# Weight sums of the values' block product: from VectorE to accumulating DMAs in DRAM

## The chip, the cores and the metric

The kernel runs on one core of one Trainium2 chip. Such a core has TensorE (PE in the profile; PEld are its weight loads), VectorE (DVE), ScalarE (ACT), GpSimd (POOL) and SyncE (SP, which here only issues DMAs). Its working memory is SBUF; the matmul results stand in PSUM; weights and intermediate sums that are not in SBUF stand in DRAM. The metric is the device time of one execution in microseconds, lower is better; one execution is also profiled, and every row shown below is of that one.

## The reference, cut to what matters

One layer of a streaming encoder: 512 frames of 1024 numbers, all in float32. One combined projection of the normed input feeds attention (q, k, v), a recurrent branch (xr, gr) and two gates (ga, gb):

```python
xn = rmsnorm(h, norm_mix_g[l])
u = jnp.einsum('bsd,de->bse', xn, w_in[l])
q, k, v, xr, gr, ga, gb = jnp.split(u, splits, axis=-1)
ya = chunked_band_attention(q, k, v, rel_table[l]) @ w_attn_out[l]
xc = causal_depthwise_conv(xr, conv_w[l], conv_b[l])
hr = rg_lru(xc, ...)
yb = (hr * jax.nn.gelu(gr)) @ w_rnn_out[l]
...
h = h + (g_a * ya + g_b * yb) @ w_o[l]
...
h = h + (jax.nn.silu(g) * up) @ w_ffn_out[l]
```

The change concerns `v`, the product of `xn` (512 x 1024) with the 1024 columns of `w_in` for the values.

## The kernel before

**Split numbers.** Every float32 operand of a product is held as two parts, a high one (rounded to TensorE's fast float32 form) and a low one, the rest. `split` (L84 to L87) makes them: ACT writes the high part (L86), DVE subtracts it from the source (L87). A product is three matmuls (`mm3`, L80 to L82): high by high, high by low, low by high.

**Weights.** The weights arrive in chunks, in the order of a list (`plan`). A chunk is loaded by SP into "raw" tiles of 512 KB, of which there are three buffers, and split into "whl" tiles, of which there are four. `weights(name, ahead)` gives a chunk and loads and splits as many as `ahead` further ones. An SP load whose buffer is not free waits at SP, and everything behind it on SP waits too.

**Order of work.** Where nothing else is said, a planner decides the order of the instructions on each engine, by what it expects to be ready; each engine then runs its own list strictly in order. `tc.keep_in_program_order(x)` ties one instruction behind the instruction that was written just before it on its engine; those written after it are not tied. In the values' product and in attention, PE's order is as written.

**The stages around the change.**

- The recurrent loop, `for j in range(0, KT, 2)`, runs over j = 0, 2, 4, 6. Each pass handles two feature tiles: the products xr and gr, the convolution (`rnn_conv`, its POOL part is L764, which writes the low half of `xch`), the gate products `rg` (L793, which read `xch`), the gates and the scan (`gates_of`, its POOL parts are L817 and L831, the low half of the recurrent output), and the products ga and gb, whose gate is applied by ACT (`gate`, into `ta` and `zB`). After j = 2, 4, 6 `sums_kept` (L319 to L340) loads blocks of other weights, sums them on DVE and stores the sums to DRAM for later stages.
- Then q and k tiles of the first heads, and the output projection of the recurrent branch, `yb` (eight products, the result into `zB` at L1152). Between them stand the scores of heads 0 and 1 (L1076 to L1087) and `x_sums` (L979, L981), which forms four sums of blocks of `xn` for the values' product.
- Then the values' product, `v_all`: the 2 x 2 blocks of `xn` and of the values' weights are multiplied by a scheme of seven block products in place of eight. Weights of three of them are blocks as they are (`w11`, `w22`, `w21`), and of four are sums of blocks (`t1` to `t4`). The seven run in the order w11, t1, t2, w22, t3, w21, t4, each 24 matmuls of 512 columns. The results are kept, added (L1032) and split again.
- Then attention over 16 heads, the merge, the product with `w_o`, and the feed-forward part.

**The sums before the change.** With the blocks B11, B12, B22, B21 of the values' weights, in two halves u = 0, 1 of 128 x 1024 numbers each: `v_weight_sums(u)`, called in the `yb` loop after its products j = 3 and j = 5, loads B11, B12 and B22 (`v_raw`, L283, two DMAs of 256 KB to a tile) and forms t1 = B12 - B11 (L291) and t2 = B22 - t1 (L292) on DVE, into SBUF tiles that stay. `v_weights` takes t1 and t2 from there; for t3 it loads B11 again and subtracts it from t2 (L306); for w21 it also turns t2 into t4 = B21 - t2 in place (L310).

A like scheme by DMAs stands in the kernel for the last stage already: `out_copy` (L224) copies a block within DRAM from SP, `out_add` (L233) adds another to it by an accumulating DMA from POOL, sometimes after a POOL copy of one column (L230) that makes POOL wait for some other engine's result.

Of the kernel before, what the change touches and what calls it, by code (L numbers as in the profile page):

```python
# [8 lines left out]
F32 = mybir.dt.float32  # L9
F32R = mybir.dt.float32r  # L10
AF = mybir.ActivationFunctionType
ALU = mybir.AluOpType
PSUM = bass.MemoryType.PSUM

P = 128
D = 1024
S = 512
KT = D // P
NT = S // P
# [10 lines left out]
C_Q, C_K, C_V, C_XR, C_GR, C_GA, C_GB = (i * D for i in range(7))  # L30
# [12 lines left out]
def block_kernel(ctx: ExitStack, tc: tile.TileContext, x, norm_mix_g, w_in, b_merge, rel_table,  # L43
# [230 lines left out]
        high_first(hl[:, 0], hl[:, 1], raw[:])  # L274
        return lambda part, k, at=every: hl[:, part, k, at]

    v_t1, v_t2 = [], []

    def v_raw(kind, kh, half, u):
        raw = wp.tile([P, 2, S], F32, tag="raw", bufs=3, name=f"raw_v_{kind}_{kh}{half}{u}")  # L280
        at = kh * S + u * CW
        for n, gr in enumerate(v_groups[half]):
            sp.dma_start(out=raw[:, :, n * CW:(n + 1) * CW],  # L283
                         in_=w_in[at:at + CW, C_V + gr * CW:C_V + (gr + 1) * CW].rearrange("(k p) e -> p k e", p=P))
        return raw[:]

    def v_weight_sums(u):

        b11, b12, b22 = v_raw("t", 0, 0, u), v_raw("t", 0, 1, u), v_raw("t", 1, 1, u)
        t1, t2 = (aw.tile([P, 2, S], F32, tag="v", bufs=4, name=f"v_t{n}_{u}")[:] for n in (1, 2))  # L290
        dve.tensor_sub(t1, b12, b11)  # L291
        dve.tensor_sub(t2, b22, t1)  # L292
        v_t1.append(t1)
        v_t2.append(t2)

    def v_weights(kind):

        hl = [wp.tile([P, 2, 2, S], F32R, tag="whl", bufs=4, name=f"whl_v_{kind}_{u}") for u in range(2)]
        for u in range(2):
            if kind == "t1":  # L300
                src = v_t1[u]
            elif kind in ("t2", "t4"):
                src = v_t2[u]
            elif kind == "t3":
                src = v_raw(kind, 0, 0, u)
                tc.keep_in_program_order(dve.tensor_sub(src, v_t2[u], src))  # L306
            else:
                src = v_raw(kind, int(kind[1]) - 1, int(kind[2]) - 1, u)
                if kind == "w21":
                    dve.tensor_sub(v_t2[u], src, v_t2[u])  # L310
            split(hl[u][:, 0], hl[u][:, 1], src)
        return lambda part, k: hl[k // 2][:, part, k % 2]

# [453 lines left out]
    def rnn_conv(j, po_xr):  # L767
        xc = conv_in(j, po_xr)
        conv_taps(j, po_xr, xc)
        return xc, conv_out(j, xc)  # L770
# [67 lines left out]
    def gates_of(j):  # L838
        pos = [rnn_gate_products(j + c, conv[j + c][1], ("s", "mm")[c]) for c in range(2)]
        for c in range(2):  # L840
            xc, _, g = conv.pop(j + c)
            held.append(rnn_gates(j + c, xc, pos[c], g))
        act.activation(u_pairs[-1][:], u_pairs[-1][:], AF.Sqrt, scale=-1.0)
        while held:
            rnn.append(rnn_scan(*held.pop(0)))

    def tile_of(name, c, tag="mm", ahead=1):

        whl = weights(name, ahead)
        if (name, c) in first:  # L850
            po = first[name, c]
            project(po, whl, c, xnT, 256, S)
        else:
            po = mm_tile(f"po_{name}_{c}", tag)
            project(po, whl, c, xnT)
        return po
# [13 lines left out]
    def gate(w, j):  # L870
        po = tile_of(f"g{'ab'[w]}{j - j % 2}", j % 2, "t" if j < 2 and w == 0 else "mm")
        act.activation((ta, zB)[w][j], po[:], AF.Tanh, bias=hb[:, 16 + 8 * w + j:17 + 8 * w + j], scale=0.5)
# [20 lines left out]
    for j in range(0, KT, 2):  # L893
        if j:
            for c in range(2):
                conv[j + c] = rnn_conv(j + c, tile_of(f"xr{j}", c, ahead=2))
        for c in range(2):
            if j:
                po = tile_of(f"gr{j}", c, "t")
                conv[j + c] += (rnn_gelu(j + c, po),)  # L900
        if j:
            gates_of(j)
        for w in range(j // 4, 2):
            for c in range(2):
                gate(w, j + c)
            if j == w == 0:
                gates_of(j)
        if j:
            sums_kept(obp, "oof"[j // 2 - 1], (0, 1, 0)[j // 2 - 1])

# [52 lines left out]
    def x_block(half, kh, part):  # L963
        return xn_all[:, 4 * kh:4 * kh + 4, part, half * 256:half * 256 + 256]

    def x_sums():

        s, s3 = (zp.tile([P, 4, 256], F32, tag="late", bufs=2, name=f"v_s{n}")[:] for n in (1, 3))
        out = {}

        def parted(key, src):
            pl, tag = (aw, "v") if key == "s4" else (aw2, "pt")
            hi, lo = (pl.tile([P, 4, 256], F32R, tag=tag, bufs=4, name=f"v_{key}{n}") for n in "hl")
            split(hi[:], lo[:], src)
            out[key] = hi, lo

        def chain(dst, first_, *rest):
            (op, one, two) = first_
            tc.keep_in_program_order(op(dst, one, two))  # L979
            for op, one in rest:  # L980
                op(dst, dst, one)  # L981

        add, sub = dve.tensor_add, dve.tensor_sub
        chain(s, (add, x_block(1, 0, 0), x_block(1, 1, 0)), (add, x_block(1, 0, 1)), (add, x_block(1, 1, 1)))
        parted("s1", s)
        chain(s, (sub, s, x_block(0, 0, 0)), (sub, x_block(0, 0, 1)))
        parted("s2", s)
        chain(s3, (sub, x_block(0, 0, 0), x_block(1, 0, 0)), (add, x_block(0, 0, 1)), (sub, x_block(1, 0, 1)))
        chain(s, (sub, x_block(0, 1, 0), s), (add, x_block(0, 1, 1)))
        return out, parted, s, s3  # L990

    def v_pairs(gr, half):
# [12 lines left out]
    def v_all(sums):  # L1005
        out, parted, s, s3 = sums
        x_, y_ = ([mm_tile(f"v_{n}{a}", tag) for a in range(2)] for n, tag in (("x", "mm"), ("y", "t")))
        z_ = [mm_tile(f"v_z{a}") for a in range(2)]

        def product(banks, kind, rows, start):  # L1010
            w = weights(f"v_{kind}")
            for a in range(2):
                for k in range(4):
                    if isinstance(rows, str):
                        hi, lo = (o[:, k, a * P:(a + 1) * P] for o in out[rows])
                    else:
                        hi, lo = (x_block(*rows, part)[:, k, a * P:(a + 1) * P] for part in range(2))
                    mm3(banks[a][:], hi, lo, w(0, k), w(1, k), start and k == 0, k == 3, parts=True)

        def keep(o, banks):  # L1020
            for a in range(2):
                act.activation(o[:, a], banks[a][:], AF.Copy)

        def given(half, side, src):
            for a in range(2):
                for n, gr in enumerate(v_groups[side]):
                    v = vs[gr][2 * half + a]
                    split(v[:, :, 0::3], v[:, :, 1:3], src(a)[:, n * CW:(n + 1) * CW].rearrange("p (a b d) -> p a b d", a=2, b=2))

        def summed(o, banks, half, side):  # L1030
            for a in range(2):
                dve.tensor_add(o[:, a], banks[a][:], o[:, a])  # L1032
            for gr in v_groups[side]:
                v_pairs(gr, half)
            given(half, side, lambda a: o[:, a])

        product(x_, "w11", (0, 0), True)
        keeps = [rnp.tile([P, 2, 2, S], F32, tag="big", bufs=4, name=f"v_keep{n}") for n in range(2)]
        v_big.append(rnp.tile([P, 2, 2, S], F32R, tag="big", bufs=4, name="v_big"))
        x1, x2, z1 = keeps[0][:, 0], keeps[0][:, 1], keeps[1][:, 0]  # L1040
        keep(x1, x_)
        product(z_, "t1", "s1", True)
        keep(z1, z_)
        parted("s4", s)
        product(x_, "t2", "s2", False)
        keep(x2, x_)
        parted("s3", s3)
        product(z_, "w22", "s4", False)
        summed(x2, z_, 0, 1)
        product(x_, "t3", "s3", False)  # L1050
        summed(z1, x_, 1, 1)
        product(y_, "w21", (0, 1), True)
        summed(x1, y_, 0, 0)
        product(x_, "t4", (1, 1), False)
        for gr in v_groups[0]:
            v_pairs(gr, 1)
        given(1, 0, lambda a: x_[a][:])
# [87 lines left out]
    for j in range(KT):  # L1145
        if j in (4, 6):
            probs[j // 2 - 2] = scores(j // 2 - 2)
        po = mm_tile(f"po_yb{j}")
        project(po, weights(f"yb{j - j % 2}"), j % 2, rnn)
        if j in (3, 5):  # L1150
            v_weight_sums(j // 2 - 1)
        dve.scalar_tensor_tensor(zB[j], zB[j], 1.0, po[:], ALU.add, ALU.mult)  # L1152
    with tc.manual_schedule(engines={mybir.EngineType.PE}):
        v_all(sums)
# [582 lines left out]
```

## Time and profile before

| what | us |
|---|---|
| median of three runs | 847.26 |
| lowest and highest of the three | 846.86, 848.89 |
| the profiled execution | 848.82 |
| its span, first to last instruction | 847.0 |
| TensorE busy in the span | 837.2 |
| VectorE busy | 654.1 |
| ScalarE busy | 524.3 |
| GpSimd busy | 159.9 |

The rows that follow are of the profile's page and of answers of its trace. A row of a group of instructions gives line, engine, operation, output and inputs by the program's names, the count, the durations in ns, and the first and last start in us. A row of a timeline gives start and duration in us; in brackets stands how long the engine was idle before, and what ended that. "SPq" is the issue of a DMA by SP, not its transfer; the "landing" is the time from the issue until the data have arrived. A row by stretches gives, for each engine, busy time and count of instructions, then the granted TensorE clock, the busy share of the 16 DMA engines and the GB/s they moved.

### The profile page before, as it was taken

The page shows a single profiled execution, that of the slowest core. Times are in us where ns is not written, and L with a number is a line of the kernel's source. Part 1 is how long each engine was busy: PE and PEld are TensorE (multiplying, and loading weights), DVE is VectorE, ACT ScalarE, POOL GpSimd, SP SyncE. Part 2 cuts the span into 40 slices and gives each one's busy share as a digit, 9 for nine tenths or more (in the row PEclk, how much of TensorE's full clock was granted, in tenths as well). Part 3 has the DMA queues.
Part 4 walks back from the last instruction along what each step waited for, and adds up shares of the span by engine and source line. Part 5 has one row for each costly group of instructions (what it writes and reads, how often), then busy time and mean ns, then how long its engine had stood idle before and what let it go on. Part 6 is the DMA issues. An engine that isn't in the chain of part 4 may idle for free.

```text
span 847.0 us, 11664 instructions
## 1 busy us (share of the span) xinstructions
PE 837.2 (99%) x4102; PEld 708.8 (84%) x4102; DVE 654.1 (77%) x960; ACT 524.3 (62%) x868; POOL 159.9 (19%) x207
## 2 busy tenths in 40 slices
PE   9999999999999999999999999999999999999996
PEld 6988888888878888888888888888888999988885
DVE  6667779886999778777568777889777878599784
ACT  7595848773456678878544469663765466555543
POOL 2412030221040043343211000005102322200000
PEclk9999999999999999999999999999999999999998
DMA  8433386687565444549448984555955576455442
GB/s 286 166 103 117 130 298 243 212 271 243 167 205 150 132 134 148 157 152 223 94 132 211 320 294 154 157 187 166 229 176 159 150 187 207 140 177 168 160 165 99
DMA packets 104058, 153.96 MB, mean 182 GB/s; under 512 B 8024, under 2 KB 62896, under 8 KB 103488
## 3 DMA queue, kind: packets, MB, share of 16 engines
q1 hardware_dynamic: 99040, 141.32, 51.2%
q0 software_dynamic: 3728, 8.96, 6.4%
q10 hardware_dynamic: 1232, 2.95, 0.9%
q8 instruction: 32, 0.52, 0.3%
q14 instruction: 26, 0.21, 0.1%
HBM read 139.53 MB, written 30.45 MB: 201 GB/s over the span
## 4 chain that ended last, share of the span: by engine, by line
PE 84%; DVE 7%; ACT 4%; DMA 3%; issue 2%; ACTq 0%; DVEq 0%
PE fu_x L80 2%; PE fu_x L81 2%; PE fu_x L82 2%; PE o L1122 2%; PE fg_x L82 2%; PE fg_x L80 2%; PE fg_x L81 2%; PE pT L1102 2%; PE po_ga L82 2%; PE po_ya L80 2%; PE po_ya L82 2%; PE p_out L81 2%; PE p_out L80 2%; PE po_ya L81 2%; PE p_out L82 2%
## 5 line engine op out<-in xcount | busy, mean ns | idle before, releaser
L1326 POOL TENSOR_TENSOR sg<-sg,keep_fu_x 128x512 f32<-128x512 f32 (+1 forms) x10 | 17.8, 1784 | 163.4 <-DVE keep_fu_x L1325 163.4
L1091 POOL TENSOR_SCALAR p<-p,rl 128x128 f32<-128x128 f32 (+3 forms) x61 | 43.8, 733 | 13.7 <-DVE rl L1087 9.4
L1085 DVE CUSTOM_DVE_ANT_0 p<-s,bias 128x128 f32<-128x128 f32 (+1 forms) x64 | 28.6, 486 | 12.6 <-PE s L1077 11.1
L1086 ACT ACTIVATE p<-p,m 128x128 f32<-128x128 f32 (+1 forms) x64 | 35.5, 555 | 2.3 <-DVE m L1085 2.0
L87 DVE TENSOR_TENSOR whl_fu_w<-raw_fu_w,whl_fu_w 128x1024 fp32r<-128x1024 f32 (+1 forms) x18 | 22.1, 1230 | 9.0 <-ACT whl_fu_w L86 9.0
L87 DVE TENSOR_TENSOR pp<-pT,pp 128x384 fp32r<-128x384 f32 (+1 forms) x48 | 26.9, 595 | 2.0 <-ACT pp L86 1.8
L81 PE MATMUL po_xr<-xnT,whl_xr 128*128 128x512 f32 (+1 forms) x80 | 27.7, 354 | 0.0
L87 DVE TENSOR_TENSOR whl_fu_t<-t_fu,whl_fu_t 128x1024 fp32r<-128x1024 f32 (+1 forms) x18 | 23.2, 1293 | 5.9 <-ACT whl_fu_t L86 5.7
L81 PE MATMUL po_gr<-xnT,whl_gr 128*128 128x512 f32 (+1 forms) x80 | 27.5, 347 | 0.0
L82 PE MATMUL po_gr<-xnT,whl_gr 128*128 128x512 f32 (+1 forms) x80 | 27.3, 347 | 0.0
L82 PE MATMUL po_xr<-xnT,whl_xr 128*128 128x512 f32 (+1 forms) x80 | 27.3, 347 | 0.0
L80 PE MATMUL po_gr<-xnT,whl_gr 128*128 128x512 f32 (+1 forms) x80 | 27.2, 347 | 0.0
L738 POOL MEMSET bias<- 64x64 f32 x16 | 2.5, 155 | 130.7 <-DMA bias<-ext_d 130.7
L80 PE MATMUL po_xr<-xnT,whl_xr 128*128 128x512 f32 (+1 forms) x80 | 26.3, 352 | 0.4 <-ACT xnT L649 0.4
L86 ACT ACTIVATE whl_fu_w<-raw_fu_w 128x1024 fp32r<-128x1024 f32 (+1 forms) x18 | 17.7, 987 | 13.0 <-issue 7.1
L80 PE MATMUL po_k<-xnT,whl_qk 128*128 128x512 f32 x64 | 25.5, 398 | 0.0
L80 PE MATMUL po_q<-xnT,whl_qk 128*128 128x512 f32 x64 | 25.5, 398 | 0.0
L80 PE MATMUL po_ga<-xnT,whl_ga 128*128 128x512 f32 x64 | 25.5, 398 | 0.0
L80 PE MATMUL po_gb<-xnT,whl_gb 128*128 128x512 f32 x64 | 25.3, 395 | 0.0
L86 ACT ACTIVATE whl_fu_t<-t_fu 128x1024 fp32r<-128x1024 f32 (+1 forms) x18 | 17.7, 989 | 12.2 <-PE fu_x L82 8.9
L82 PE MATMUL po_ga<-xnT,whl_ga 128*128 128x512 f32 x64 | 25.1, 392 | 0.1
L81 PE MATMUL po_q<-xnT,whl_qk 128*128 128x512 f32 x64 | 25.0, 390 | 0.0
(610 smaller groups left out, 3036.8 us busy)
## 6 DMA issues: line engine op xcount, KB each, us to landing
raw_qk<-in_w_in_dram SPq DMA_DIRECT2D x32, 256.0 KB, 3.3
out_t<-in_w_ffn_out_dram SPq DMA_DIRECT2D x16, 512.0 KB, 5.5
raw_fu_w<-in_w_ffn_in_dram SPq DMA_DIRECT2D x16, 512.0 KB, 4.7
raw_fo<-in_w_ffn_out_dram SPq DMA_DIRECT2D x14, 512.0 KB, 4.3
raw_t<-out_t SPq DMA_DIRECT2D x24, 256.0 KB, 3.3
raw_xr<-in_w_in_dram SPq DMA_DIRECT2D x8, 512.0 KB, 6.0
raw_gr<-in_w_in_dram SPq DMA_DIRECT2D x8, 512.0 KB, 4.5
raw_ga<-in_w_in_dram SPq DMA_DIRECT2D x8, 512.0 KB, 4.9
```

What stands on the lines that cost most here:

```text
L80: pe.matmul(o, sh, mh, start=start, stop=False, skip_group_check=parts)
L81: pe.matmul(o, sh, ml, start=False, stop=False, skip_group_check=parts)
L82: pe.matmul(o, sl, mh, start=False, stop=stop, skip_group_check=parts)
L86: act.activation(hi, src, AF.Copy)
L87: dve.tensor_sub(lo, src, f(hi))
L738: pool.memset(b[64:128, 448:512], NEG)
L1085: dve.tensor_tensor_reduce(prob[qb][:], scs[qb][:, 0:w], bias[:, S - w:S], -1.0, 3e38, ALU.add, ALU.min, nmax[:, qb:qb + 1])
L1086: act.activation(prob[qb][:], prob[qb][:], AF.Exp, bias=nmax[:, qb:qb + 1], scale=-1.0, accum_out=lsum[:, qb:qb + 1])
L1091: eng.tensor_scalar(prob[qb][:], prob[qb][:], rl[:, qb:qb + 1], 1.0, ALU.mult, ALU.mult)
L1102: pe.transpose(pt[:, at * P:(at + 1) * P], prob[qb][:, kb * P:(kb + 1) * P], ident[:])
L1122: pe.matmul(po[:, S - n:S], st, pp[i][:, part, lo:lo + n], start=kb == 0 and part == 0, stop=kb == NT - 1 and part == 1)
L1326: (pool if keep and (unit != f_units[-1] or side) else dve).tensor_mul(o, o, keep[a] if keep else banks[a])
```

## The change

The sums are made in DRAM, with signs turned so that only additions are needed: `t1` starts as a copy of block (0, 1) and adds block (0, 0); `t2` as a copy of block (1, 1) and adds t1; `t3` as a copy of block (1, 1) and adds block (0, 1); `t4` as a copy of block (1, 0) and adds t2. `x_sums` and `summed` change signs to match, with the same count of instructions.

Each kind stands in two DRAM tiles of 512 KB (n = 0, 1, one for each group of 256 columns). There are eight copies on SP, four after the gates of pass j = 0 (t1, t3) and four after those of j = 2 (t2, t4). There are twelve accumulating DMAs on POOL: t1 and t3 in halves (eight of 256 KB), t2 and t4 whole (four of 512 KB). In each of the passes j = 2, 4, 6 four are issued: one after each of the two `rnn_conv`, and one after each of the two gb gates, there behind a one-column POOL copy of the gate's result `zB`. A hook in the `yb` loop would issue what is left. `v_weights` loads t1 to t4 as it loads the plain blocks: into raw tiles, by two DMAs of 256 KB each. The DVE sums, their SBUF tiles and the loads that fed them are gone.

```diff
-    v_t1, v_t2 = [], []
+    v_t = {(kind, n): dr.tile([P, 4, CW], F32, name=f"v_{kind}_{n}") for kind in ("t1", "t2", "t3", "t4") for n in range(2)}
+
+    def v_rows(kh, half, n):
+        col = C_V + v_groups[half][n] * CW
+        return w_in[kh * S:kh * S + S, col:col + CW].rearrange("(k p) e -> p k e", p=P)
+
+    def v_copy(kind, n):
+
+        block = {"t1": (0, 1), "t2": (1, 1), "t3": (1, 1), "t4": (1, 0)}[kind]
+        tc.keep_in_program_order(sp.dma_start(out=v_t[kind, n][:], in_=v_rows(*block, n)))
+
+    def v_add(kind, n, k, after=None):
+
+        if after is not None:
+            cell = cp.tile([P, NT], F32, tag="lsum", bufs=2, name=f"cell_v{kind}{n}_{k.start}")
+            tc.keep_in_program_order(pool.tensor_copy(cell[:, 0:1], after))
+        one = v_t[kind, n][:]
+        two = v_rows(0, int(kind == "t3"), n) if kind in ("t1", "t3") else v_t["t1" if kind == "t2" else "t2", n][:]
+        tc.keep_in_program_order(pool.dma_start(out=one[:, k], in_=two[:, k], accum_op=ALU.add, max_dma_last_dim=4096))
+
+    v_copies = [(kind, n) for kind in ("t1", "t3", "t2", "t4") for n in range(2)]
+    v_adds = [(kind, n, k) for kind in ("t1", "t3", "t2", "t4") for n in range(2)
+              for k in ((slice(0, 2), slice(2, 4)) if kind in ("t1", "t3") else (slice(0, 4),))]
+
+    def v_next(after=None):
+
+        if v_adds:
+            v_add(*v_adds.pop(0), after=after)
...
-    def v_weight_sums(u):
...
     def v_weights(kind):
...
-            if kind == "t1":
-                src = v_t1[u]
-            elif kind in ("t2", "t4"):
-                src = v_t2[u]
-            elif kind == "t3":
-                src = v_raw(kind, 0, 0, u)
-                tc.keep_in_program_order(dve.tensor_sub(src, v_t2[u], src))
+            if kind[0] == "t":
+                src = wp.tile([P, 2, S], F32, tag="raw", bufs=3, name=f"raw_v_{kind}_{u}")[:]
+                for n in range(2):
+                    sp.dma_start(out=src[:, :, n * CW:(n + 1) * CW], in_=v_t[kind, n][:, 2 * u:2 * u + 2])
             else:
                 src = v_raw(kind, int(kind[1]) - 1, int(kind[2]) - 1, u)
-                if kind == "w21":
-                    dve.tensor_sub(v_t2[u], src, v_t2[u])
             split(hl[u][:, 0], hl[u][:, 1], src)
...
                 conv[j + c] = rnn_conv(j + c, tile_of(f"xr{j}", c, ahead=2))
+                v_next()
...
                 gate(w, j + c)
+                if j and w:
+                    v_next(zB[j + c][:, 0:1])
             if j == w == 0:
                 gates_of(j)
+        for what in v_copies[:4] if j < 4 else ():
+            v_copy(*v_copies.pop(0))
...
-        chain(s, (add, x_block(1, 0, 0), x_block(1, 1, 0)), (add, x_block(1, 0, 1)), (add, x_block(1, 1, 1)))
+        chain(s, (sub, x_block(1, 0, 0), x_block(1, 1, 0)), (add, x_block(1, 0, 1)), (sub, x_block(1, 1, 1)))
...
-        chain(s, (sub, x_block(0, 1, 0), s), (add, x_block(0, 1, 1)))
+        chain(s, (add, x_block(0, 1, 0), s), (add, x_block(0, 1, 1)))
...
-        summed(x2, z_, 0, 1)
+        summed(x2, z_, 0, 1, dve.tensor_sub)
         product(x_, "t3", "s3", False)
-        summed(z1, x_, 1, 1)
+        summed(z1, x_, 1, 1, dve.tensor_sub)
...
-        if j in (3, 5):
-            v_weight_sums(j // 2 - 1)
+        if j % 2 == 0 and j < 4:
+            v_next()
```

More of the change, by code (lines that the diff above doesn't have):

```diff
@@ L285, in v_raw @@
         return raw[:]
-    def v_weight_sums(u):
[L289 to L294, printed above, removed]
     def v_weights(kind):
@@ L1028, in given, with summed @@
                     split(v[:, :, 0::3], v[:, :, 1:3], src(a)[:, n * CW:(n + 1) * CW].rearrange("p (a b d) -> p a b d", a=2, b=2))
-        def summed(o, banks, half, side):
+        def summed(o, banks, half, side, op=dve.tensor_add):
             for a in range(2):
-                dve.tensor_add(o[:, a], banks[a][:], o[:, a])
+                op(o[:, a], *((o[:, a], banks[a][:]) if half else (banks[a][:], o[:, a])))
             for gr in v_groups[side]:
```

## The prediction

> **What bounds the kernel now.** I read the page first, for the shares of the engines:
>
> ```profile
> span 847.0 us, 11664 instructions
> ## 1 busy us (share of the span) xinstructions
> PE 837.2 (99%) x4102; PEld 708.8 (84%) x4102; DVE 654.1 (77%) x960; ACT 524.3 (62%) x868; POOL 159.9 (19%) x207
> ```
>
> TensorE (PE) is busy for 837.2 of 847.0 us. Nothing in the diff touches a matmul, so the change can win only where PE stands still today, and can lose wherever it makes PE stand still. So the next view is the busy time by stretches, cut at the stages that the change touches:
>
> ```profile
> core 0: us, PE busy (x) PEld busy (x) DVE busy (x) ACT busy (x) POOL busy (x), PEclk, DMA share, GB/s
> 40.00:100.00 60.00, 60.00 (x274) 48.67 (x273) 41.57 (x50) 47.39 (x63) 10.53 (x9) 1.00 0.36 108
> 100.00:160.00 60.00, 60.00 (x270) 49.19 (x269) 50.31 (x54) 37.95 (x50) 15.27 (x10) 1.00 0.77 270
> 160.00:220.00 60.00, 60.00 (x273) 49.31 (x272) 46.73 (x51) 35.20 (x47) 10.06 (x11) 1.00 0.65 217
> 220.00:260.00 40.00, 38.92 (x171) 31.18 (x170) 36.28 (x49) 22.40 (x36) 10.24 (x10) 1.00 0.60 187
> 260.00:500.00 240.00, 240.00 (x1215) 205.40 (x1214) 182.78 (x360) 154.44 (x316) 53.31 (x89) 1.00 0.63 182
> ```
>
> In the recurrent loop and the first q/k tiles (40 to 220) PE never stops, nor from 260 to 500. Between 220 and 260, where the recurrent output projection ends and the block product of the values begins, PE is idle for 40.00 - 38.92 = 1.08 us, while VectorE (DVE) is busy for 36.28 of 40 us. The timeline of PE shows the largest of these stops:
>
> ```profile
> 244.09 0.39 PE L80 MATMUL v_x<-whl_v_w,xnT 128*128 128x512 f32 x1
> 244.57 0.50 PE L81 MATMUL v_x<-whl_v_w,xnT 128*128 128x512 f32 x1
> 244.91 0.40 PE L82 MATMUL v_x<-whl_v_w,xnT 128*128 128x512 f32 x1
> ```
> ```profile
> 249.92 0.39 PE L80 MATMUL v_z<-whl_v_t,v_s1h 128*128 128x512 f32 x1
> 251.05 0.50 PE L81 MATMUL v_z<-whl_v_t,v_s1h 128*128 128x512 f32 x1 [0.75 <-DVE whl_v_t L87]
> 251.39 0.40 PE L82 MATMUL v_z<-whl_v_t,v_s1l 128*128 128x512 f32 x1
> 251.63 0.39 PE L80 MATMUL v_z<-whl_v_t,v_s1h 128*128 128x512 f32 x1
> ```
>
> A running matmul starts 0.23 us after the one before (251.39 to 251.63 is 0.24). Here the steps are 0.48 and 0.34 us, then 1.13 and 0.34: too much by 0.25 + 0.11 + 0.90 + 0.11 = 1.4 us. At 251 the releaser is DVE's low half (L87) of the second weight tile of t1. Why are these halves late? SyncE's (SP's) queue, VectorE's sums and ScalarE's (ACT's) wait tell it:
>
> ```profile
> 222.48 8.79 SPq L283 DMA_DIRECT2D raw_v_t<-in_w_in_dram  x6
> 231.37 0.41 SPq L737 DMA_DIRECT2D bias<-ext_d  x1
> 231.82 0.61 SPq L224 DMA_DIRECT2D out_t<-in_w_ffn_out_dram  x1
> 234.41 0.38 SPq L283 DMA_DIRECT2D raw_v_w<-in_w_in_dram  x1
> ```
> ```profile
> L291 DVE TENSOR_TENSOR v_t<-raw_v_t,raw_v_t x2: 1220/1220/1221, 218.4 to 233.2; 128x1024 f32<-128x1024 f32 x2
> L292 DVE TENSOR_TENSOR v_t<-raw_v_t,v_t x2: 1220/1222/1225, 221.2 to 236.1; 128x1024 f32<-128x1024 f32 x2
> L306 DVE TENSOR_TENSOR raw_v_t<-v_t,raw_v_t x2: 1214/1216/1217, 257.4 to 261.6; 128x1024 f32<-128x1024 f32 x2
> L310 DVE TENSOR_TENSOR v_t<-raw_v_w,v_t x2: 1222/1224/1226, 263.4 to 266.2; 128x1024 f32<-128x1024 f32 x2
> ```
> ```profile
> ACT whl_v_w L86 <- DMA raw_v_w<-in_w_in_dram: 8.6, 2, 8.1
> ```
>
> Six loads of the sums' blocks hold the three "raw" buffers until VectorE has summed (the second L291 starts at 233.2). Only then, at 234.41, can the first tile of w11 be loaded; ACT waits 8.1 us for it, and the product starts with its splits late.
>
> **The change part by part.**
>
> Removed: eight DVE subtractions, 2 each at L291, L292, L306 and L310, 8 x 1.22 = 9.8 us, of which 4 x 1.22 = 4.9 us lie before 238; and the loads that held the buffers. Then w11's loads can go out where the sums' six stand from 222.48 on, up to 12 us earlier. DVE's 36.28 of 40 us falls to about 32. The stops at 244 and 251 go: -1.4 us. The bounds: nothing, if other DVE work is what comes last, and -2.2 us: the idle 1.08 us plus, for each of about four stops, the 0.16 us by which matmuls overlap (0.39 long, 0.23 apart) and 0.11 us of restart. What is next after that is PE itself.
>
> Added in the same place: t1, t2, t3 and t4 are now loaded from DRAM, 16 loads of 256 KB, where 16 went away, but w11 to t4 are now fourteen raw tiles in a row through three buffers.
>
> ```profile
> raw_v_t<-in_w_in_dram SPq DMA_DIRECT2D x16, 256.0 KB, 3.3
> L224 SPq DMA_DIRECT2D out_t<-in_w_ffn_out_dram x16: 547/554/1467, 231.8 to 392.1; - x16
> L233 POOL DMA_DIRECT2D out_t<-in_w_ffn_out_dram x8: 1032/1046/1107, 379.4 to 460.8; - x8
> L233 POOL DMA_DIRECT2D out_t<-out_t x8: 809/822/850, 591.8 to 688.0; - x8
> DMA to landing us min/median/max: 5.3/6.1/9.6
> ```
>
> One round of a buffer is two issues (2 x 0.4 us), 3.3 us to land, 1.06 us on ACT and 1.22 us on DVE: 6.4 us, or 2.1 us a tile with three buffers. PE takes a tile per 12 matmuls, 12 x 0.23 = 2.7 us. So it fits, at 0, with 0.6 us of cover a tile; the cover is gone when a landing takes over 5 us.
>
> Added on SP: eight copies of 512 KB inside DRAM (four in pass j=0, four in j=2), like L224: 8 x 0.55 = 4.4 us of issue. They wait for nothing, but loads of gr2 and gr4 queue behind them. Four copies in a row, each bounded by 3.3 us (a load of half the size) and 9.6 us (the slowest row here), would be 13 to 38 us one after the other; they share 16 engines that are busy for 0.36 of the time from 40 to 100. I take the lower end, for that share. The cover is that weights are fetched one to two chunks ahead, and a chunk is 48 matmuls x 0.23 = 11 us. So zero on the path, and a few us if a late load has only one chunk of cover; the accumulating transfers, which come where the share is 0.77 already (100 to 160), stand under the same cover.
>
> Added on POOL: twelve accumulating DMAs, eight like the first L233 row (256 pieces each, at half the bytes) and four like the second: 8 x 1.05 + 4 x 0.82 = 11.7 us, and six one-column copies of 0.2 to 1.1 us. POOL is busy for 36 of the 180 us from 40 to 220. Each pass of j = 2, 4, 6 has four hooks, 12 in all for 12 adds, so the hook in the projection loop finds nothing left. What stands behind these on POOL decides. In the profile of before:
>
> ```profile
> 438.39 1.05 POOL L233 DMA_DIRECT2D out_t<-in_w_ffn_out_dram  x1
> 439.51 0.20 POOL L230 COPY cell_t<-mT 128x1 f32<-128x1 f32 x1
> 444.87 1.04 POOL L233 DMA_DIRECT2D out_t<-in_w_ffn_out_dram  x1 [5.16 <-issue]
> ```
> ```profile
> 109.01 4.71 POOL L831 TENSOR_TENSOR rnn<-u,rnn 128x512 fp32r<-128x512 f32 x2 [14.23 <-ACT rnn L830]
> 115.30 1.76 POOL L764 TENSOR_TENSOR xch<-xc,xch 128x512 fp32r<-128x512 f32 x1 [1.58 <-ACT xch L763]
> ```
> ```profile
> 150.08 2.55 POOL L831 TENSOR_TENSOR rnn<-u,rnn 128x512 fp32r<-128x512 f32 x2 [7.73 <-ACT rnn L830]
> 152.96 1.91 POOL L764 TENSOR_TENSOR xch<-xc,xch 128x512 fp32r<-128x512 f32 x1 [0.33 <-ACT xch L763]
> 159.04 1.29 POOL L764 TENSOR_TENSOR xch<-xc,xch 128x512 fp32r<-128x512 f32 x1 [4.17 <-issue]
> ```
> ```profile
> 127.08 1.66 PE L793 MATMUL rg<-xch,wrg 64*128 64x512 f32 x12
> 161.53 1.66 PE L793 MATMUL rg<-xch,wrg 64*128 64x512 f32 x12
> ```
>
> The second DMA of a pair goes out 444.87 - 438.39 = 6.5 us after the first, with no releaser shown: POOL stands until the first has landed. Two of the four hooks of a pass are queued behind the pair of L831, that is just ahead of the next pass's L764, whose result PE's gate products (L793) read at 127.08 and 161.53. In my forecast POOL's order or the earlier landing of half-size transfers leaves those in time: 0 on the path.
>
> [...]
>
> [...]
>
> Sum: 0 + 0 + 0 - 1.4. The profiled execution took 848.8 us (848.82, 1.8 us outside the span); by it the changed kernel takes 847.4. It lies 1.6 us above the median of the three runs, 847.26, so on the median the forecast is 845.9.
>
> **The rivals.**
>
> (1) POOL holds the gate products up; this is the one that ends slower. With a pause S between two DMAs of 256 pieces: L831 ends at 152.63, a cell of 0.2, DMA at 152.8, the next at 152.8 + S. If L764 stands behind both, then comes the third (0.82 us, itself waiting until 152.8 + 2S) and the second L764 (1.29): done at 154.9 + 2S. PE needs that at 161.5 + 10 x 0.12 = 162.7, so it decides from S = 3.9 us. In pass j = 4 the same count from 113.7 gives 116.2 + 2S against 128.2, from S = 6.0. At S = 6.5 the loss is 5.2 + 1.0 = 6.2 us, net +4.8: 852.1 us. At S = 5 it is 2.2, net +0.8: 848.1. For it: the wait at 444.87, and 0.33 us of room before L764 at 152.96. Against it: POOL idles most of the loop, half the bytes, and PE's order in this loop is the planner's, which may set gb's matmuls ahead of L793. Chance 0.22 for the full loss, 0.10 for the mild one.
>
> (2) The three raw buffers become the wait: at landings of 5.6 us instead of 5.0 each of 14 tiles is late by 0.2 us, 2.8 in all, net +1.4: 848.7 us. For it: ACT waits 8.1 us for w11 today; against it: landings of 3.3 us, at a DMA share of 0.60. Chance 0.10, of which 0.04 slower than the bound below.
>
> (3) The stops only get a new releaser: 36 us of 40 leaves DVE late for scores, key sums or the splits anyway, and the time stays at 847.3. For it: DVE's share; against it: the row that names what came last (L87 at 251.05) belongs to the splits that were started late. Chance 0.14.
>
> **How the numbers follow.** The forecast of 845.9 has 0.44. A measurement of this kernel can tell about 0.3%, 2.5 us, from no change. Faster than 844.7 needs more than the bound of 2.2 us, so only the scatter of the medians gives it: 0.05, out of the forecast's 0.44. Slower than 849.8: 0.22 + 0.04 = 0.26. Between: 0.69. The range runs from 844.6 to 851.5: below it I leave 0.05, above it the worse part of rival 1, some 0.13.
>
> **What would show it.** Right: PE busy for 40 of 40 us where the values' product starts; the first load of w11 issued before about 228; L291, L292, L306 and L310 gone from DVE; L793 with no wait in passes 4 and 6. Rival 1: an idle time of PE ahead of L793 with POOL's xch as releaser, and POOL's xch starting just behind a DMA. Rival 2: ACT's high halves waiting for raw tiles loaded from DRAM sums, and PE waiting for them. The forecast is wrong if PE loses time at any place where it stands at 60.00 of 60.00 today, or if the planner reorders the loop so that other work on DVE comes late.

## The result and the profile after

| | median us | from, to | runs |
|---|---|---|---|
| before, beside it | 848.83 | 846.86 to 852.13 | 6 |
| after | 858.46 | 858.12 to 861.18 | 6 |

The changed kernel is slower by 1.2%: ratio 1.012, 95% interval 1.0096 to 1.0144. Its profiled execution took 858.54 us, 9.7 more than the profiled execution of before (848.82). In the new line numbers the lines named in the prediction stand 13 to 18 higher: xch L777 (was 764), rg L806 (793), rnn L844 (831), f_t L346 (333), f_b's copy on ACT L350 (337), zb L1170 (1152); the accumulating DMA is L295, its one-column copy L292.

The engines' shares on the page, then the busy time by the same stretches as before (stretch, busy us of each engine, granted clock of PE, share of the DMA engines, GB/s):

```profile
span 856.7 us, 11704 instructions
PE 840.5 (98%) x4102; PEld 710.7 (83%) x4102; DVE 651.5 (76%) x952; ACT 525.4 (61%) x868; POOL 171.7 (20%) x225
```
```profile
100.00:160.00 60.00, 57.28 (x250) 46.49 (x249) 49.11 (x53) 36.58 (x47) 19.86 (x17) 0.97 0.87 277
160.00:220.00 60.00, 55.86 (x244) 44.82 (x243) 43.59 (x44) 33.67 (x46) 17.06 (x16) 0.98 0.90 255
220.00:260.00 40.00, 40.00 (x181) 33.27 (x180) 34.59 (x48) 20.25 (x33) 8.05 (x13) 0.99 0.51 146
```

Where PE had stood still, from 220 to 260, it is now busy for 40.00 of 40.00 us (the same work now stands some 11 us later; from 260 to 500 PE is busy throughout too). Where it had never stood still, from 100 to 220, it loses 2.72 + 4.14 us. Two more things are in these rows: the granted clock falls below 1.00 there, and DVE is less busy than before. (Over the span DVE's busy time falls from 654.1 to 651.5 us, though subtractions of 9.8 us went: one split of `whl_qk`, at 164.81 us, takes 5.11 us where the others take 1.2.)

The timeline of PE shows the first stop (start, length, engine, line, operation; in brackets the idle time before it and what ended it):

```profile
127.08 1.43 PE L806 MATMUL rg<-xch,wrg 64*128 64x512 f32 x10
131.22 0.50 PE L806 MATMUL rg<-xch,wrg 64*128 64x512 f32 x2 [2.71 <-POOL xch L777]
...
132.32 0.63 PE L82 MATMUL po_gb<-xnT,whl_gb 128*128 128x512 f32 x1
132.75 0.63 PE L80 MATMUL po_gb<-xnT,whl_gb 128*128 128x512 f32 x1
133.17 0.63 PE L81 MATMUL po_gb<-xnT,whl_gb 128*128 128x512 f32 x1
...
135.31 0.49 PE L80 MATMUL po_gb<-xnT,whl_gb 128*128 128x512 f32 x1
135.63 0.40 PE L81 MATMUL po_gb<-xnT,whl_gb 128*128 128x512 f32 x1
...
168.88 0.50 PE L806 MATMUL rg<-xch,wrg 64*128 64x512 f32 x2 [1.15 <-POOL xch L777]
...
212.78 0.39 PE L82 MATMUL po_yb<-rnn,whl_yb 128*128 128x512 f32 x1
216.16 0.47 PE L80 MATMUL po_yb<-rnn,whl_yb 128*128 128x512 f32 x1 [2.99 <-DVE zb L1170]
```

Three stops, at 131, 169 and 216 us. The first costs more than its idle time: behind it, from 132.3 to 135.3, a matmul starts 0.43 us after the one before (132.75 to 133.17) and not 0.23; the same stands behind the third, not behind the second. Two windows show that it is the clock, 0.51 and 0.52 of full speed:

```profile
132.00:135.50 3.50, 3.50 (x10) 2.71 (x9) 3.50 (x5) 3.41 (x7) 1.16 (x1) 0.51 1.10 346
217.50:221.00 3.50, 3.50 (x10) 2.70 (x9) 2.67 (x4) 3.31 (x6) 0.76 (x2) 0.52 0.77 257
```

The bill: a stop costs its excess over a normal step (2.87, 1.31 and 3.15 us), 0.1 to 0.3 us of restart, and, behind the first and third, eight matmuls that each take 0.2 us too long, 1.6 us. That is 4.8 + 1.6 + 4.9 = 11.3 us. Against it stand the stops of 1.95 us (small steps included) that are gone from 231 to 251. Net 9.4 of the 9.7 us. PE's order of matmuls is the same in both kernels, so the starts can also be compared one by one: against an execution of the kernel before that has none of these stops (e6, below), the three cost 4.6, 1.7 and 4.9 us.

POOL's timeline names the cause of the first two:

```profile
113.81 1.13 POOL L295 DMA_DIRECT2D v_t<-in_w_in_dram  x1
114.58 1.35 POOL L292 COPY cell_vt<-zb 128x1 f32<-128x1 f32 x1
121.88 1.15 POOL L295 DMA_DIRECT2D v_t<-in_w_in_dram  x1 [5.95 <-PE po_gr L82]
122.59 1.76 POOL L777 TENSOR_TENSOR xch<-xc,xch 128x512 fp32r<-128x512 f32 x1
128.71 1.15 POOL L295 DMA_DIRECT2D v_t<-in_w_in_dram  x1 [4.36 <-PE rg L806]
129.47 1.69 POOL L777 TENSOR_TENSOR xch<-xc,xch 128x512 fp32r<-128x512 f32 x1
...
157.08 1.18 POOL L295 DMA_DIRECT2D v_t<-in_w_in_dram  x1
...
164.26 1.14 POOL L295 DMA_DIRECT2D v_t<-in_w_in_dram  x1 [5.76 <-ACT g L793]
164.97 1.75 POOL L777 TENSOR_TENSOR xch<-xc,xch 128x512 fp32r<-128x512 f32 x1
166.21 1.33 POOL L295 DMA_DIRECT2D v_t<-v_t  x1
```

The second DMA of a pair goes out 8.07 us behind the first (113.81 to 121.88), the third 6.83 us behind that, and both xch stand behind a pause. The releasers in these brackets (PE, ACT) only happened to finish something shortly before; in e1, below, the second DMA of a pair doesn't wait for them, with the same instructions in the same order. What POOL waits for has no row of its own, but the landings fit. The DMA issued at 113.81, by itself:

```profile
DMA to landing us min/median/max: 7.7/7.7/7.7
```

It lands at 121.5, and the next goes out at 121.88. That one lands 6.5 us after its issue, at 128.4 (the next: 128.71), and the one of 157.08 after 6.9 us, at 164.0 (the next: 164.26). Note the last line: the DMA at 166.21 did not wait for the one issued 1.95 us before. It is a sum of two DRAM tiles, of 128 pieces, where the others have 256 (packets on POOL's queue: 288 for the two sums from 197 to 210 us, 272 for the one DMA of 157.08 to 164, so 16 more than the pieces for each). So it isn't "one DMA at a time", and the first theory, a guess at this point, was a room that holds only so many pieces at once.

The third stop has another chain. DVE's and ACT's timelines:

```profile
205.51 1.21 DVE L87 TENSOR_TENSOR whl_yb<-raw_yb,whl_yb 128x1024 fp32r<-128x1024 f32 x1
212.94 1.23 DVE L351 TENSOR_TENSOR f_b<-f_b,f_b 128x1024 fp32r<-128x1024 f32 x1 [6.21 <-ACT f_b L350]
214.08 1.22 DVE L87 TENSOR_TENSOR whl_yb<-raw_yb,whl_yb 128x1024 fp32r<-128x1024 f32 x1
215.33 0.69 DVE L1170 SCALAR_TENSOR_TENSOR zb<-zb,po_yb 128x512 f32<-128x512 f32 x1
```
```profile
200.62 1.05 ACT L86 ACTIVATE whl_yb<-raw_yb 128x1024 fp32r<-128x1024 f32 x1
211.84 1.06 ACT L350 ACTIVATE f_b<-f_b 128x1024 fp32r<-128x1024 f32 x1 [10.17 <-DMA f_t<-f_b]
```

PE waits for zb, zb stands on DVE behind f_b's low half, that waits for ACT's copy, and ACT waits 10.17 us until the store of f_t has landed, because it overwrites what is being stored. Before, the wait was 4.93 us:

```profile
199.36 1.06 ACT L337 ACTIVATE f_b<-f_b 128x1024 fp32r<-128x1024 f32 x1 [4.93 <-DMA f_t<-f_b]
```

The DMA view from 180 to 222 us (KB each, us from issue to landing; for the queue: packets, MB, share of the 16 engines) tells why:

```profile
q0 software_dynamic: 288, 1.05, 14.7%
...
f_t<-f_b SPq DMA_DIRECT2D x4, 512.0 KB, 8.7
...
v_t<-v_t POOLq DMA_DIRECT2D x2, 512.0 KB, 8.0
```

The two adds of t4, issued at 197.41 and 199.26, take 14.7% of 42 us, that is 6.2 us of all sixteen engines, just where the three stores (issued 201.4 to 204.5) want them. These land 8.5 to 9.2 us after issue; in the profile of before the same stores land in 3.8 to 4.9 us.

**Theory 1**: two causes add up. (M1) POOL stands still when a DMA's pieces don't fit in this room beside those in flight, and xch waits behind it: 6.4 us. (M2) t4's adds delay f_t's stores, ACT, DVE and zb: 4.9 us. **Theory 2**: the traffic of copies and adds as such slows the loop. **Theory 3**, on M2 alone: the third stop is only a consequence of the loop being late by 6.4 us already.

### The profile page after: what moved, and what is told of

Read it like the earlier page. It is cut to its first block, busy times and chain, and to the rows that moved or that the text cites. A ratio compares the mean times of both kernels' runs of the same rounds, so it can differ in the third digit from the quotient of the medians.

```text
span 856.7 us, 11704 instructions
## 1 busy us (share of the span) xinstructions
PE 840.5 (98%) x4102; PEld 710.7 (83%) x4102; DVE 651.5 (76%) x952; ACT 525.4 (61%) x868; POOL 171.7 (20%) x225
## 4 chain that ended last, share of the span: by engine, by line
PE 87%; DVE 4%; ACT 3%; DMA 3%; issue 2%; POOL 0%; ACTq 0%; DVEq 0%; POOLq 0%
PE o L1140 2%; PE fu_x L81 2%; PE fu_x L82 2%; PE fg_x L80 2%; PE fg_x L82 2%; PE fg_x L81 2%; PE fu_x L80 2%; PE pT L1120 2%; DMA f_t<-f_b 2%; PE po_ga L82 2%; PE po_ya L82 2%; PE po_ya L80 2%; PE po_ya L81 2%; PE p_out L82 2%; PE p_out L80 2%; PE p_out L81 2%
## 5 line engine op out<-in xcount | busy, mean ns | idle before, releaser
L1109 POOL TENSOR_SCALAR p<-p,rl 128x128 f32<-128x128 f32 (+3 forms) x61 | 40.5, 680 | 16.5 <-DVE rl L1105 12.3
L80 PE MATMUL po_yb<-rnn,whl_yb 128*128 128x512 f32 x64 | 25.7, 402 | 3.0 <-DVE zb L1170 3.0
L87 DVE TENSOR_TENSOR whl_qk<-raw_qk,whl_qk 128x1024 fp32r<-128x1024 f32 x16 | 23.4, 1470 | 5.3 <-ACT whl_qk L86 5.3
L80 PE MATMUL po_gb<-xnT,whl_gb 128*128 128x512 f32 x64 | 25.8, 404 | 0.0
L82 PE MATMUL po_gb<-xnT,whl_gb 128*128 128x512 f32 x64 | 25.6, 400 | 0.0
L81 PE MATMUL po_gb<-xnT,whl_gb 128*128 128x512 f32 x64 | 25.6, 400 | 0.0
L82 PE MATMUL po_yb<-rnn,whl_yb 128*128 128x512 f32 x64 | 25.6, 399 | 0.0
```

Of the source, the lines that this page charges most:

```text
L80: pe.matmul(o, sh, mh, start=start, stop=False, skip_group_check=parts)
L81: pe.matmul(o, sh, ml, start=False, stop=False, skip_group_check=parts)
L82: pe.matmul(o, sl, mh, start=False, stop=stop, skip_group_check=parts)
L87: dve.tensor_sub(lo, src, f(hi))
L1109: eng.tensor_scalar(prob[qb][:], prob[qb][:], rl[:, qb:qb + 1], 1.0, ALU.mult, ALU.mult)
```

## The experiments

The first four ran together; before beside them took 848.06 us (26 runs).

**e1: more room.** The number is bytes per partition; a tile that only fills space gives them up (112 float32 numbers, 448 bytes). The expectation takes these bytes for room for the DMAs' descriptors; no run shows what stands in them. Nothing else differs; the order of the instructions on each engine is the same.

```diff
-    top.tile([P, 120], F32, name="top_fill")
+    top.tile([P, 8], F32, name="top_fill")
-    ... dynamic_dma_scratch_size=1024)
+    ... dynamic_dma_scratch_size=1472)
```

> The same program with more room for the descriptors of POOL's DMAs (1472 bytes per partition in place of 1024; a filler tile gives up the space). Theory 1, POOL's pause: two accumulating DMAs of 256 KB then stand in the room together, the pauses of 6.0 and 4.4 us ahead of the xch subtractions go, and with them PE's stops at 131 us (3.1 us and 1.6 us of half-speed matmuls) and at 169 us (1.6 us): 858.5 - 6.3 = 852.2 if the stop at 216 us (4.9 us) stays because t4's adds still crowd the queues, 847.3 if that stop is only a consequence of the late loop. Theory 2, the traffic of the copies and adds as such slows the loop: the traffic is the same, 858.5 within 0.5.

Measured: 849.98 us, ratio to before 1.0033 (1.0018 to 1.0048), between the two times that were expected (852.2 and 847.3). POOL's timeline of e1, and PE's only stop in the loop:

```profile
116.17 1.14 POOL L295 DMA_DIRECT2D v_t<-in_w_in_dram  x1
...
117.92 1.13 POOL L295 DMA_DIRECT2D v_t<-in_w_in_dram  x1
118.63 1.73 POOL L777 TENSOR_TENSOR xch<-xc,xch 128x512 fp32r<-128x512 f32 x1
```
```profile
209.94 0.47 PE L80 MATMUL po_yb<-rnn,whl_yb 128*128 128x512 f32 x1 [0.98 <-DVE zb L1170]
```

The pair goes out 1.75 us apart, not 8.07, and both stops at rg are gone with the same traffic: theory 2 falls as the cause of these two, M1 stands. The third stop stays, though the loop isn't held up any more, but it is only 1.1 us long and without the slow matmuls. (This execution was also 2 us late 31 us into the span, ahead of every add. So was e11's, and e12's by 0.4 us; these three, the ones with more room, lose most of it at 17 to 21 us, where e1's PE waits for a split of gr's weights; no other execution loses time there. Whether the room has to do with it is open.)

**e2 and e3: adds left out.**

```diff
     v_adds = [(kind, n, k) for kind in ("t1", "t3", "t2", "t4") for n in range(2)
-              for k in (... else (slice(0, 4),))]
+              for k in (... else (slice(0, 4),))][:0]     # e2
+              for k in (... else (slice(0, 4),))][:10]    # e3
```

> Leaves out all twelve accumulating DMAs (the copies and the loads stay, so the sums are not made). Theory 1 (POOL's pause) and the crowding by t4's adds together: all three stops (4.8 + 1.6 + 4.9 us) go and the gain at the values' product stays: 858.5 - 11.3 = 847.2. If the copies on SP or the shared raw buffers carry part of the loss, the time stays above 849 and a stop is left that the other runs also show.

> Leaves out only the last two accumulating DMAs, those of t4 at 197 and 199 us. If their traffic is what makes the stores of f_t land 9 us after issue, and through ACT, DVE and zb stops PE at 216 us, that stop goes and the two others stay: 858.5 - 4.9 = 853.6. If the third stop comes from the loop being late alone, it stays: 858.5 within 0.5.

Measured: e2 847.15 us (ratio 0.9996, 0.9983 to 1.0008), e3 853.44 us (1.0072, 1.0059 to 1.0085). Both as theory 1 has them, 847.2 and 853.6. In e3, PE's first stop at rg and the landing of f_t's stores:

```profile
131.89 0.59 PE L806 MATMUL rg<-xch,wrg 64*128 64x512 f32 x2 [3.40 <-POOL xch L777]
```
```profile
DMA to landing us min/median/max: 4.3/4.3/4.6
```

The stores land in 4.3 us again, and PE has no stop at zb although the loop is just as late as in the changed kernel (6.3 us behind e6 in both). Theory 3 falls: a late loop without t4's adds doesn't stop at zb, a loop that isn't held up with them (e1) does. By these runs M1 costs 853.44 - 847.15 = 6.3 us and M2 858.46 - 853.44 = 5.0 us. But the two don't simply add up. Where M1 alone is taken away, in e1, the time falls by 8.5 us and not 6.3, since the third stop is short there: M2's 5.0 us is its price in a loop that M1 has made late, and whether it is the lateness that makes it so long isn't shown. The eight copies and the loads of DRAM sums, which e2 keeps, cost nothing that can be measured.

**e4: the adds where POOL is idle.** All twelve are kept. The hooks move behind the second xch, behind the second a and behind the second rnn of a pass.

```diff
                 conv[j + c] = rnn_conv(...)
-                v_next()
+            v_next(f(conv[j + 1][1][:, 1])[:, 0:1])
+            v_next()
...
             held.append(rnn_gates(...))
+        if j:
+            v_next(held[-1][2][:, 0:1])
+            if j == 2:
+                v_next()
...
             rnn.append(rnn_scan(...))
+        if j >= 2:
+            v_next(f(rnn[-1][:, 1])[:, 0:1])
...
-                if j and w:
-                    v_next(zB[j + c][:, 0:1])
```

> All twelve adds are kept, but stand on POOL where the profile shows it idle for 8 to 15 us: two behind the second xch of a pass, one or two behind the second a, one behind the second rnn. Theory 1: no pause stands ahead of an xch, and t4's adds are issued some 15 us before the stores of f_t, so all three stops go: 847.2. Theory 2 (traffic as such): the same bytes in the same loop, 858.5 within 1. Third way: the pause now holds up an a or an rnn and the stop moves: 850 to 856, with PE waiting for rnn or rg by POOL L830 or L844.

Measured: 848.83 us, ratio 1.0015 (1.0001 to 1.0029), with single times from 847.3 to 850.9 and one of 853.7. Its profiled execution (847.26) has none of the three stops, and POOL still pauses 5.9 us between two adds, with nothing urgent behind. The median lies 1.6 us above the 847.2 expected.

**e5, e6, e7, e8: which stops come back.** The kernel before twice more, e4 once more, and e4 with t4's adds put back to the end of the loop.

> The kernel before, profiled a second time, to see whether PE's stops at the values' product (231, 244 and 251 us, 1.4 us in the first profile with the smaller steps beside them 1.95 us) stand in every execution. If they are a property of the kernel they are there again and the time is 848.8; if they come and go with the landing of the raw loads, a run near 846.7 lacks them, and the gain of the change is that much smaller on the median.

> The kernel before, profiled a third time, as in e5_before_again: the same stops at 231, 244 and 251 us if they belong to the kernel, others or none if they follow the landing of loads.

> The kernel of e4_moved, profiled a second time, since its times spread from 847.3 to 850.9 while its profiled execution was the fastest of them. If the spread comes from the start (loads ahead of the first matmuls) PE is late from 9 to 25 us on; if adds still collide with the loop's loads, a stop stands between 75 and 216 us that the first profile does not have.

> e4_moved with the two adds of t4 put back behind the gates of the last pass, as in the changed kernel; the ten others stay moved, so that the loop is on time. If t4's adds crowd the stores of f_t by themselves, those land about 9 us after issue, ACT's copy of f_b waits some 9 to 10 us, and PE stops at about 209 us by 1 to 3.4 us, the longer with half-speed matmuls behind it: 848.5 + 1.1 to 4.9 = 849.6 to 853.4. If the third stop needs the late loop too, no stop stands there and the time is that of e4_moved, 847.3 to 848.8.

The kernel before took 847.43 and 847.34 us in e5 and e6. The stretch from 220 to 260, first in e5, then in e6:

```profile
220.00:260.00 40.00, 39.78 (x178) 32.69 (x177) 37.13 (x50) 23.32 (x37) 12.88 (x10) 1.00 0.61 186
```
```profile
220.00:260.00 40.00, 40.00 (x180) 33.23 (x179) 35.04 (x48) 23.63 (x37) 10.53 (x10) 1.00 0.59 179
```

The stops that the prediction set out to remove (1.08 us of idle time there) are 0.22 us in one and absent in the other. They belong to some executions of the kernel before, not to the kernel. On the median the change had about 1 us to win: e2, without adds, is 0.9 us below the before beside it, and e9, further on, 1.1, hardly outside the noise.

e7 took 848.83 us, and PE has two stops that e4's first profile lacks:

```profile
207.01 0.47 PE L80 MATMUL po_yb<-rnn,whl_yb 128*128 128x512 f32 x1 [0.26 <-DVE zb L1173]
213.37 0.47 PE L80 MATMUL po_yb<-rnn,whl_yb 128*128 128x512 f32 x1 [0.67 <-DVE q L958]
```

Same chain, smaller: f_b's subtractions start at 196.19 there against 192.11 in e5. e8 took 851.36 us (848.5 to 856.5), 2.5 us more than e4 for nothing but the place of two DMAs (3.4 us if each is taken against the before beside it, ratios of 1.0055 and 1.0015). Profiled at 848.52:

```profile
204.17 1.06 ACT L350 ACTIVATE f_b<-f_b 128x1024 fp32r<-128x1024 f32 x1 [9.74 <-DMA f_t<-f_b]
```
```profile
208.49 0.47 PE L80 MATMUL po_yb<-rnn,whl_yb 128*128 128x512 f32 x1 [1.57 <-DVE zb L1175]
```

So t4's adds delay ACT by the full amount in a loop that is on time. How much of that reaches PE differs from run to run.

**e9 and e10: t4's adds behind yb.** There POOL is idle, and the DMA engines were busy for 0.25 to 0.37 of the time in e7.

```diff
         dve.scalar_tensor_tensor(zB[j], zB[j], 1.0, po[:], ALU.add, ALU.mult)
+        if j in (0, 1):
+            v_next(zB[j][:, 0:1], last=True)    # the last two adds wait for this
```

> e4_moved with the two adds of t4 put behind the first two products of yb, where POOL is idle from 215 to 235 us and the DMA engines are busy 0.25 to 0.37 of the time in e7_moved_again. If what is left of the loss in e4_moved is t4's adds beside the loads of f_b at 170 to 195 us, PE's stops at 207 and 213 us (0.42 and 0.83 us in e7_moved_again) go: 847.0 to 847.5, level with the kernel before, whose repeated profiles keep only 0.4 us of the stops that the change removes. If the ten other adds crowd the loop's loads too, it stays at 848.8.

> The kernel of e8_t4_late, profiled a second time: its times fall into 848.5 to 849.9 and 852.8 to 856.5. If a stop of PE over about 3 us brings matmuls at half speed behind it (as in the three stops of 3.1 to 3.8 us so far, and not behind those of 1.1 to 2.0 us), a run near 853 shows a longer stop at 208 us with some eight matmuls of 427 ns behind it, and one near 849 a shorter stop without them.

Measured: e9 846.87 us against 847.93 of before, ratio 0.9991 (0.9982 to 0.9999). Over the whole stretch that was in question PE never stops:

```profile
100.00:160.00 60.00, 60.00 (x270) 49.16 (x269) 49.93 (x53) 36.70 (x48) 22.13 (x19) 1.00 0.96 294
160.00:220.00 60.00, 60.00 (x273) 49.28 (x272) 47.76 (x51) 37.35 (x50) 15.81 (x17) 1.00 0.77 243
220.00:260.00 40.00, 40.00 (x181) 33.23 (x180) 31.91 (x46) 23.54 (x37) 7.97 (x10) 1.00 0.64 189
```

The DMA engines are busier than in the changed kernel (0.96 against 0.87 from 100 to 160) and PE doesn't mind: again not the traffic, but what stands beside it. e10 took 849.13 us, with a stop of 1.4 us at 208 and no slow matmuls. No execution near 853 was profiled, so what the slower half of e8's times is made of stays open. One hint: in these three (852.8, 853.0 and 856.5 us) the mean granted clock is 0.993 to 0.994, in the three fast ones 0.998 to 0.999, so slow matmuls seem to be a part of it.

**e11 and e12: the smallest mends.** e11 is e1 with 1088 bytes; e12 is e11 with t4's adds as in e9 and the ten others where the change has them.

> As e1_ring, but with only 64 bytes per partition more than the changed kernel (1088 in place of 1024). In the changed kernel a DMA of 256 pieces waits for the one of 256 pieces ahead of it, and one of 128 pieces behind one of 256 does not; so the room holds 1.5 such DMAs and not 2. If two just miss fitting, a little more is enough: the pauses in pairs go and the time is that of e1_ring, 849 to 851. If the room that two need is nearer to 1472, the pauses and both stops stay: 858.5 within 1. [...]

> The changed kernel with the smallest mend of both causes: 64 bytes more room, and t4's two adds behind the first two products of yb as in e9_t4_yb; the ten other adds stay where the change has them. If the two causes are all of the loss, no stop stands at 131, 169 and 216 us and the time is that of e9_t4_yb, 846.7 to 847.5. If the room is too small, 853.4 as in e3_no_t4_adds; if the ten adds in their old places crowd the loop, 848.5 to 850.

Measured: e11 852.43 us (1.0046, 1.0030 to 1.0062), e12 848.61 us (1.0005, 0.9996 to 1.0014). POOL's timeline and PE's stop in e11:

```profile
116.01 1.14 POOL L295 DMA_DIRECT2D v_t<-in_w_in_dram  x1
116.89 2.35 POOL L295 DMA_DIRECT2D v_t<-in_w_in_dram  x1
117.60 2.96 POOL L777 TENSOR_TENSOR xch<-xc,xch 128x512 fp32r<-128x512 f32 x1
124.80 1.15 POOL L295 DMA_DIRECT2D v_t<-in_w_in_dram  x1 [4.24 <-ACT xch L776]
```
```profile
212.24 0.47 PE L80 MATMUL po_yb<-rnn,whl_yb 128*128 128x512 f32 x1 [2.76 <-DVE zb L1170]
```
```profile
212.00:216.00 4.00, 3.76 (x17) 3.15 (x18) 2.25 (x5) 2.48 (x5) 0.61 (x1) 1.00 0.96 291
```

The last row shows that the clock stays at 1.00 behind this stop. With 64 bytes more the pause inside a pair (8.07 us) is gone: the pair goes out 0.88 us apart. The third still waits (4.24 us of idle time ahead of it). So two DMAs of 256 pieces don't fit in 1024 bytes per partition and fit in 1088; if only the pieces count, and evenly, an estimate from these two runs is 2.00 to 2.13 bytes for a piece. These starts agree with it: in the changed kernel 256 + 128 pieces (768 to 816 bytes) find room in 1024, and a further 128 don't; that one goes out at 169.29, just behind the landing of the DMA of 164.26 (4.7 us after its issue, at 169.0). In pass 6 256 + 256 + 128 pieces (1280 to 1360 bytes) find room in e1's 1472, where the third goes out 1.95 us behind the second (157.24 to 159.19), and not in e11's 1088, where it takes 5.70 us (157.26 to 162.96). That is what M1 was: two DMAs missed fitting by a hair, 64 of 1024 bytes at the most. That nothing but the pieces takes up room is an assumption that no run tests by itself. e11 lies above the expected 849 to 851 because its third stop is 2.9 us long and this execution too was 2.2 us late 31 us into the span. e12 lies above the expected 846.7 to 847.5, in the range (848.5 to 850) that was set for ten adds that crowd the loop. Its profiled execution, the fastest at 847.26, has no stop of PE in the loop, but the times run from 847.3 to 849.7; the difference to e9, 1.7 us, is in no profile taken here, and that rival stays open for it.

## Why the prediction was wrong

It gave 845.9 (844.6 to 851.5), with most of its chance on no measurable change; the result is 858.46, slower. By its steps:

- **"In my forecast POOL's order or the earlier landing of half-size transfers leaves those in time: 0 on the path."** This is the step that failed first, by 6.3 us (e3 against e2; gone in e1). Neither half held. POOL's order put both DMAs of the pair ahead of the first xch and the third between the two, just as rival 1 had written it down. And half the bytes did not land earlier: pauses of 8.07, 6.83 and 7.18 us, where the row of 512 KB in the profile of before showed 6.5. Rival 1's count was right for pass 4: it has the second xch ready at 116.2 us plus two pauses, 116.2 + 8.07 + 6.83 = 131.1, and PE went on at 131.22. It should have been the forecast: the 6.5 us was measured and the room of 0.33 us ahead of L764 was measured, while the hope against them had no row. Its price of 6.2 us comes close to the 6.3, but that is luck. It had 1.0 us for pass 4 and 5.2 for pass 6; the stops cost 4.6 (1.6 of it slow matmuls, the rest pauses longer than 6.5) and 1.7. In pass 6 it made the second xch wait for two pauses, and there was only one: the third DMA, of 128 pieces, went out at 166.21 without a pause. Its 852.1 us misses 858.46 above all by the second cause, which no rival had.
- **"The accumulating transfers ... stand under the same cover."** The cover of one to two chunks is that of weights fetched ahead. It held for them: in none of these profiles does PE, once the adds have begun, wait in the loop for a weight. But the prediction never asked who else uses the DMA engines with a wait behind it. f_t's stores do: ACT waited 4.93 us for them already before, and DVE, zb and PE stand behind ACT with little room. The two adds of t4 lengthened that wait to 10.17 us: 5.0 us (e3), and 2.5 us on the median when they alone are late (e8 against e4).
- **"The stops at 244 and 251 go: -1.4 us."** The mechanism is right: w11's load goes out at 219.25 in e4, with the loop on time, and at 226.20 in the changed kernel's late one (before: 234.41), and PE is busy for 40.00 of 40 us. The size is that of one execution. Two more of the kernel before show 0.22 and 0 us of idle time in that stretch. Without any adds (e2) the time is that of before within 0.1%, and with all of them well placed (e9) it is 0.1% less.
- **Rivals 2 and 3.** Three raw buffers for fourteen tiles never became the wait; neither they nor the copies cost anything in e2. DVE late for other work was not what limited either: there was only little left to gain.
- **The clock.** No term stood for slow matmuls behind a stop. Two of the three stops drew 1.6 us each of them, 3.2 us of the 11.3.

The sum as it was: 6.3 for POOL's pauses, 5.0 for t4's adds, less about 1 us at most for the gain: 10.3 us. The result is 9.6 us above the before beside it (848.83) and 10.4 us above the one beside e1 to e4 (848.06).

## What to carry to other kernels

Moving arithmetic off an engine that isn't the bound wins at most the bottleneck's idle time in that stage (here 1.08 us in one execution, 0.22 and 0 in two others). Look at more than one execution before you count on it. A DMA issued by a compute engine is an instruction in that engine's order, and if it may have to wait for room, whatever stands behind it waits too (here xch, behind pauses of 6.8 to 8.1 us from issue to issue, and PE with it for 2.71 us): put it where the engine has several us to spare, or make sure that two fit. And ask of each new transfer not only whether the engines have share left, but which transfers with a waiting reader or writer are in flight beside it (here f_t's stores, which land after 8.5 to 9.2 us in place of 3.8 to 4.9).

## What the runs showed of the hardware

- POOL's room: with 1024 bytes per partition a 256 KB accumulating DMA in 256 pieces waits for one of the same kind in flight, and one of 512 KB in 128 pieces doesn't. With 1088 bytes two of 256 pieces go together and a third waits. So it isn't the bytes that count; the number of pieces fits all of these. The wait carries no releaser of its own in the profile: it ended 0.3 to 0.4 us after the landing of an earlier DMA (121.5, 128.4 and 164.0 us), and the names in its brackets are of work that ended shortly before by chance.
- An accumulating DMA inside DRAM of 256 KB in 1 KB pieces took 4.7 to 7.7 us to land (median 6.5), hardly less than the 512 KB of before (5.3 to 9.6, median 6.1). The pauses ahead of the xch are 6.8 to 8.1 us from issue to issue.
- Two accumulating DMAs of 512 KB issued 2 to 7 us ahead of three stores of 512 KB on SP's queue bring their landing from 3.8 to 4.9 us (before) to 8.5 to 9.2 us; without the two it is 4.3 to 4.6 us (e3).
- After stops with 2.71 and 2.99 us of idle time (131 and 216 us in the changed kernel) seven or eight matmuls ran 0.43 us apart, with a granted clock of 0.51 and 0.52. After 0.26 to 1.57 us none did, but after 2.76 us in e11 none did either (clock 1.00 from 212 to 216). So the length of a stop alone doesn't decide it; what does, no run shows.
